# A hybrid decoder trunk on one core: the inverse's small matmuls in another order, and the first loads and token sums arranged anew

## The chip, the cores and the metric

The kernel runs on one core of a Trainium2 chip. Times are device microseconds of one execution; the time before is the median of three runs. A core has TensorE (PE; its weight loads are shown as PEld), VectorE (DVE), ScalarE (ACT), GpSimd (POOL) and SyncE (SP), which here issues nearly all loads and stores. Each engine has its own list of instructions.

## The reference

Two layers act on x of 512 tokens by 1024 features, in fp32. What one layer computes:

```python
h = rms_norm(x, norm_mix[i])
proj = einsum('bsd,dc->bsc', h, w_in[i])            # split into 15 column groups
y_a = gated_delta_net(...)       # 4 heads of 64: causal convolution over 4 tokens, chunked delta rule
y_b = mlstm(...)                 # 4 heads of 64: matrix memory with exponential gates
y_c = sliding_window_attention(q, k, v, sinks, cos, sin)   # 8 query heads, 2 kv heads, window 128
x = x + einsum('bsc,cd->bsd', concatenate([y_a, y_b, y_c]), w_out[i])
u = einsum('bsd,df->bsf', rms_norm(x, norm_mlp[i]), w_up[i])
x = x + einsum('bsf,fd->bsd', square(relu(u)), w_down[i])
gate = sigmoid(einsum('bsd,de->bse', rms_norm(x, norm_ple[i]), w_ple_gate[i]))
x = x + gate * einsum('bsk,kd->bsd', p[i], w_ple_proj[i])
# after both layers: rms_norm(x, norm_final)
```

The gated delta net solves, for each head and chunk, a unit lower triangular system with (I + strict_lower(beta k k^T * decay)), and then carries a 64 x 64 state from chunk to chunk. The attention turns the first 16 of 64 features of q and k by cos and sin of position times frequency (the rotary tables).

## The kernel before

x is kept with features on partitions, as eight tiles X of 128 features by 512 tokens. Every large fp32 product is done as three fp32r matmuls (`mm3`, lines 187 to 193): both operands are split into a rounded high part and the remainder, and high by high, high by low, low by high are added in PSUM. The weights come from HBM as raw tiles of 128 x 512, four stationary blocks each; `w_load_` (line 161) loads one (two buffers), ACT copies it to `whi` (line 167), DVE subtracts to get `wlo` (line 169). `w_ahead` and `w_next` keep two such tiles in flight. RMSNorm is applied late: the matmuls run on x times the gain, and the factor of each token (the row tile R) is multiplied in when a product leaves PSUM.

A layer goes through these sections, in program order:

- tok (lines 391 to 416): the token-major columns (values, gates). For each of 8 chunks of features, 12 matmuls of 400 columns into four PSUM tiles. In layer 0 each chunk first loads X (line 395) and splits it (line 216/217), and loads its own weight tile (`tok_weights`, line 335) through the ring of two raw buffers.
- the norm's factors: in layer 0 `token_sums` (line 220) loads x once more, token-major, in four tiles of 128 x 1024 from a pool of two, and ACT squares and sums them; `Norm.finish` (line 254) makes the reciprocal root on DVE and spreads it with four transposes to R.
- in layer 0 then `rope_tables2` (line 296): the angles, a Sin on ACT, eight transposes on TensorE, and two stores of the tables to HBM, from which section rope reads them.
- gates, rows, cols: gate functions and their running sums; conv (lines 516 to 537): six projections with the convolution; nrmk, vb, decay: norms, and the matrices At (lines 573 to 610).
- binv and dbl (lines 615 to 689): the triangular inverse of 16 blocks (4 chunks of 128 tokens by 4 heads). The 16 x 16 diagonal blocks are solved on DVE; the 32 x 32, 64 x 64 and 128 x 128 levels come from products Y - Y A Y on TensorE. The 32-level uses `t1p` and `y1p` (lines 642, 649), four quadrants of 32 rows by 16 blocks; the 64-level uses `t2p`, `y1p` and `x1p` (lines 668, 673, 676). These are plain fp32 matmuls of 32 x 32 by 32 columns; each shows as two matmul instructions.
- scan (line 694 on): the state passes through four chunks, ending in On.
- mlproj, ml, mlfin: the mLSTM; rope and swa: the attention (yc); og: output gates.
- ycb, out1, ya, out2: `out_group` (line 986) multiplies by w_out. Group one takes yc and the mLSTM's part yb (six stationary blocks for each of 8 output tiles, 144 matmuls), group two the delta net's part ya (two blocks, 48 matmuls). After group two each output tile is split for the MLP and squared for the next norm (`fin_mlp`).
- the MLP in four groups of 8 up and 8 down tiles, and the gated input embedding; the last layer ends with the final norm and the stores.

The order on each engine is not written by hand. A planner takes the instructions in program order and places each when its operands and a buffer should be ready by its model; `tc.high_priority(offset=n)` moves what stands inside it n places ahead in that order (or back, if negative). `seg(name)` applies the table `PRI`; the weight preparation has its own offset, `HPRI` = 250. Within the mixing part the big projections thus fill in between the dependent steps of the three head groups.

At the very beginning one fp32 matmul of zeros (line 137) runs on TensorE before the data are there.

Of the kernel before, what the change touches and what calls it, by code (L numbers as in the profile page):

```python
# [79 lines left out]
def trunk(ctx, tc, xT, xK, pT, posr, pos, wfm, wtm, consts, negi, smalls, gfin, out, dbg=None, depth=L):  # L80
# [51 lines left out]
    with tc.high_priority(offset=4000):  # L132
        zt = tp.tile([128, T], F32, tag="acc", name="zt", bufs=1)
        G.memset(zt, 0.0)
        pw = ps_tile([128, T], "pw")
        for _ in range(1):
            PE.matmul(out=pw, lhsT=zt[:, 0:128], rhs=zt, start=True, stop=True)
# [23 lines left out]
    def w_load_(i):  # L161
        raw = wp.tile([128, WC * 128], F32, tag="raw", name="raw", bufs=2)
        nc.sync.dma_start(out=raw, in_=wfm[i // NCH, i % NCH])
        keep = i >= total - TAILC
# [68 lines left out]
    class Norm:  # L233
# [20 lines left out]
        def finish(self, pt_=None, ps=None):  # L254
            pt_ = pt_ or ps_tile
            ps = self.sums(pt_) if ps is None else ps
            ms = pad(tp, [128, NB], "ms", "ms", 2)
            V.tensor_scalar(ms, ps, 1.0 / D, EPS, ALU.mult, ALU.add)
            rT = pad(tp, [128, NB], "rT", "rT", 2)
            rsqrt(rT, ms, [128, NB], tp, "rn")  # L260
            pr = pt_([128, T], "rb")
            for b in range(NB):
                row_of(pr[:, b * 128:(b + 1) * 128], rT[:, b:b + 1])
            R = tp.tile([128, T], F32, tag="R", name="R", bufs=1)
            A.activation(out=R, in_=pr, func=ACTF.Copy)
# [996 lines left out]
```

## Time and profile before

| what | value |
|---|---|
| median of 3 runs | 1384.7 us (1383.63 to 1391.9) |
| the profiled execution | 1385.26 us |
| its span | 1383.5 us |
| TensorE busy | 1353.4 us, 98% |
| VectorE busy | 824.5 us, 60% |
| ScalarE busy | 614.6 us, 44% |
| granted TensorE clock over the span | 0.975 |
| moved by DMA | 131.89 MB, mean 95 GB/s |

In the profile, a line such as "L642 PE MATMUL t1p<-Yd,At" names the line of the kernel, the engine, the operation, the tile written and those read. In a timeline the first number is the start and the second the length, in us from the start of the span; "x4" merges four in a row, and the brackets say how long the engine had been idle and what ended it. Matmuls overlap: one lasts longer than the distance to the next, so a rate is read from the starts. In a table by stage the busy time is that of each engine within the stage, with the number of instructions that touch it.

The mixing part of layer 0 ends at about 296 us, its MLP at about 640; the mixing part of layer 1 lies between about 700 and 972.

### The profile page before, as it was taken

How to read it: one execution, taken by the hardware profiler on the slowest of the kernel's cores; microseconds unless marked ns; L12 is line 12 of the kernel's file. 1: busy time of each engine (PE TensorE's matmuls, PEld its weight loads, DVE VectorE, ACT ScalarE, POOL GpSimd, SP SyncE). 2: the span in 40 equal slices, each digit the busy share in tenths (PEclk: the TensorE clock that was granted, in tenths of full speed). 3: DMA queues.
4: the chain of work that ended last, by engine and by line, in shares of the span. 5: the costliest groups of instructions: out<-in, count | busy, mean ns of one | idle time of the engine just before them, and what ended most of it. 6: DMA issues, size and time to landing. Idle time of an engine off the chain costs nothing.

```text
span 1383.5 us, 20187 instructions
## 1 busy us (share of the span) xinstructions
PE 1353.4 (98%) x7348; PEld 1126.2 (81%) x7348; DVE 824.5 (60%) x1751; ACT 614.6 (44%) x1245; POOL 136.3 (10%) x152
## 2 busy tenths in 40 slices
PE   8999999999999999999999999999999999999996
PEld 7778888878888888888898888887888888888886
DVE  5878768674343443455769696788534434444555
ACT  6574464353242342443544736625423424234443
POOL 1023121020000000010212231202000000000110
PEclk9999979999999999999999997999999999999998
DMA  6433311323333333333434331313333333333332
GB/s 222 122 100 88 77 35 44 107 84 99 99 95 96 99 91 100 99 92 94 146 109 115 99 80 35 90 48 98 94 98 100 92 99 99 92 99 93 98 94 90
DMA packets 89172, 131.89 MB, mean 95 GB/s; under 512 B 21600, under 2 KB 30304, under 8 KB 89072
## 3 DMA queue, kind: packets, MB, share of 16 engines
q1 hardware_dynamic: 87984, 129.55, 33.3%
q8 instruction: 58, 0.95, 0.3%
q10 hardware_dynamic: 1088, 1.05, 0.2%
q14 instruction: 42, 0.34, 0.1%
HBM read 125.02 MB, written 5.54 MB: 94 GB/s over the span
## 4 chain that ended last, share of the span: by engine, by line
PE 84%; DVE 9%; ACT 2%; DMA 2%; issue 2%; SPq 0%; DVEq 0%; ACTq 0%
PE down L191 9%; PE down L193 9%; PE down L192 8%; PE up L191 8%; PE up L192 8%; PE up L193 8%; PE proj L191 3%; PE proj L192 3%; PE proj L193 3%; PE gate L191 2%; PE gate L193 2%; PE gate L192 2%; DVE wlo L169 2%; PE outp L192 2%; PE outp L191 2%
## 5 line engine op out<-in xcount | busy, mean ns | idle before, releaser
L167 ACT ACTIVATE whi<-raw 128x512 fp32r<-128x512 f32 x404 | 253.1, 630 | 536.0 <-PE down L192 203.8
L169 DVE TENSOR_TENSOR wlo<-raw,whi 128x512 fp32r<-128x512 f32 x404 | 292.3, 725 | 179.4 <-ACT whi L167 178.6
L191 PE MATMUL down<-hidh,whi 128*128 128x512 f32 x512 | 201.7, 394 | 0.0
L192 PE MATMUL up<-xsl,whi 128*128 128x512 f32 x512 | 199.5, 390 | 2.1 <-DVE xsl L217 2.1
L193 PE MATMUL up<-xsh,wlo 128*128 128x512 f32 x512 | 199.4, 390 | 2.0 <-DVE wlo L169 2.0
L191 PE MATMUL up<-xsh,whi 128*128 128x512 f32 x512 | 199.9, 391 | 0.4 <-ACT whi L167 0.2
L193 PE MATMUL down<-hidh,wlo 128*128 128x512 f32 x512 | 199.4, 392 | 0.0
L192 PE MATMUL down<-hidl,whi 128*128 128x512 f32 x512 | 197.5, 388 | 0.0
L191 PE MATMUL proj<-xsh,whi 128*128 128x512 f32 x304 | 123.9, 407 | 1.3 <-ACT whi L167 1.1
L244 POOL TENSOR_TENSOR acc<-acc,sq 128x512 f32<-128x512 f32 x29 | 39.7, 1369 | 862.5 <-ACT sq L243 857.0
L193 PE MATMUL proj<-xsh,wlo 128*128 128x512 f32 x304 | 123.0, 405 | 0.0
L192 PE MATMUL proj<-xsl,whi 128*128 128x512 f32 x304 | 122.3, 402 | 0.0
L192 PEld LDWEIGHTS up<-xsl,whi 128*128 128x128 f32 x512 | 96.1, 188 | 23.8 <-DVE xsl L217 4.0
L193 PEld LDWEIGHTS up<-xsh,wlo 128*128 128x128 f32 x512 | 96.1, 188 | 23.0 <-DVE wlo L169 3.1
L193 PEld LDWEIGHTS down<-hidh,wlo 128*128 128x128 f32 x512 | 96.1, 188 | 22.5
L191 PEld LDWEIGHTS up<-xsh,whi 128*128 128x128 f32 x512 | 96.1, 188 | 21.7 <-ACT whi L167 1.7
L192 PEld LDWEIGHTS down<-hidl,whi 128*128 128x128 f32 x512 | 96.1, 188 | 21.5
L1056 DVE TENSOR_TENSOR X<-X,down 128x512 f32<-128x512 f32 x64 | 44.0, 687 | 115.2 <-PE down L193 115.2
L191 PEld LDWEIGHTS down<-hidh,whi 128*128 128x128 f32 x512 | 96.2, 188 | 19.3
L1047 DVE SCALAR_TENSOR_TENSOR ha<-up,R 128x512 f32<-128x512 f32 x64 | 44.0, 691 | 90.4 <-PE up L193 87.8
L191 PEld LDWEIGHTS proj<-xsh,whi 128*128 128x128 f32 x304 | 59.1, 194 | 14.3 <-ACT whi L167 1.5
L214 DVE TENSOR_TENSOR hidl<-hf,hidh 128x512 fp32r<-128x512 f32 x64 | 44.2, 691 | 42.9 <-ACT hidh L213 42.9
(362 smaller groups left out, 2182.4 us busy)
## 6 DMA issues: line engine op xcount, KB each, us to landing
raw<-wfm SPq DMA_DIRECT2D x404, 256.0 KB, 2.6
X<-xT SPq DMA_DIRECT2D x16, 256.0 KB, 3.1
raw<-wtm SPq DMA_DIRECT2D x16, 200.0 KB, 3.2
xk<-xK SPq DMA_DIRECT2D x4, 512.0 KB, 5.1
gr<-scr SPq DMA_DIRECT2D x8, 256.0 KB, 4.5
Mr<-scr SPq DMA_DIRECT2D x8, 256.0 KB, 3.4
xd<-X SPq DMA_DIRECT2D x8, 256.0 KB, 2.5
X<-xd SPq DMA_DIRECT2D x8, 256.0 KB, 2.8
```

The costliest lines, as they stand in the source:

```text
L167: A.activation(out=hi, in_=raw, func=ACTF.Copy)
L169: (G if (i % NCH) * WC < WPOOL else V).tensor_tensor(lo, raw, f(hi), ALU.subtract)
L191: PE.matmul(out=ps, lhsT=wh, rhs=ah, start=start and k == 0, stop=False)
L192: PE.matmul(out=ps, lhsT=wh, rhs=al, start=False, stop=False)
L193: PE.matmul(out=ps, lhsT=wl, rhs=ah, start=False, stop=stop and k == n - 1)
L214: V.tensor_tensor(lo, src, f(hi), ALU.subtract)
L244: (G if self.n < 6 else V).tensor_tensor(self.acc, self.acc, q, ALU.add)
L1047: V.scalar_tensor_tensor(a_t, ps, 0.0, R, ALU.max, ALU.mult)
L1056: V.tensor_tensor(X[m], X[m], ps, ALU.add)
```

## The change

Six things are done at once.

1. *Warm-up.* The zero tile is of type fp32r and set by DVE, and nine matmuls of it run instead of one.
2. *Head of layer 0.* X and the token weights are loaded at priority 2500, the token weights into eight tiles (`yq`) that are free at that time instead of the ring of two; two projection weight tiles are then loaded ahead; the token-major x comes last, in eight halves of 128 x 512 into other free tiles (`ms_`, `us`), each squared and summed by itself; DVE adds the two halves. `finish` gets two priorities, for the factors and for R.
3. *Rotary tables.* `rope_tables2` is called after the convolution, at priority -1000, instead of after the norm.
4. *Inverse by quadrants.* In the 32-level the loops are exchanged, so that matmuls in a row lie in the four quadrants in turn; in the 64-level those of the two halves alternate, with `x1p` among them, and the ACT copies of both halves come after all the matmuls.
5. *Output groups.* yb moves from the first group to the second, 96 matmuls each; the weights are packed in that order.
6. *Priorities.* The table PRI is another, mostly for layer 0, partly for layer 1. Small tiles come from a pool of their own (`mq`).

```diff
 PRI = {
-    ("tok", 0): -400, ("vb", 0): -100, ("scan", 0): -600, ("og", 0): 30, ("out1", 0): -400, ("ya", 0): -600,
-    ("nrmk", 0): -600, ("ml", 0): -100, ("conv", 0): 150, ("decay", 0): 30, ("mlproj", 0): -300,
-    ("out2", 0): -100, ("dbl", 0): 30, ("ycb", 0): -600, ("cols", 0): 150, ("gates", 0): -50, ("binv", 0): -300,
-    ("gates", 1): -300, ("cols", 1): -100, ("binv", 1): 100, ("dbl", 1): 600, ("mlproj", 1): 30, ("ml", 1): 30,
-    ("rope", 1): 200, ("og", 1): -100, ("out1", 1): -100, ("ya", 1): 400, ("out2", 1): 200, ("ycb", 1): -50,
-    ("mlfin", 1): 60, ("rows", 1): -600, ("tok", 1): 30, ("decay", 1): 30, ("swa", 1): -50,
+    ("tok", 0): 200, ("scan", 0): -200, ("og", 0): 200, ("out1", 0): -100, ("ya", 0): -50, ("nrmk", 0): 600,
+    ("rope", 0): -300, ("ml", 0): -100, ("conv", 0): 600, ("decay", 0): 200, ("mlproj", 0): 400,
+    ("out2", 0): 100, ("ycb", 0): -400, ("cols", 0): 600, ("gates", 0): 200, ("binv", 0): -300,
+    ("rows", 0): -200, ("ch", 0): 2500, ("rb", 0): 300, ("rtab", 0): -1000, ("chm", 0): 150, ("mlfin", 0): 30,
+    ("gates", 1): 400, ("cols", 1): -100, ("binv", 1): 200, ("dbl", 1): 600, ("mlproj", 1): 30, ("ml", 1): 30,
+    ("rope", 1): -400, ("og", 1): -100, ("out1", 1): 150, ("ya", 1): -400, ("out2", 1): 200, ("ycb", 1): -50,
+    ("vb", 1): -600, ("mlfin", 1): 60, ("rows", 1): -600, ("tok", 1): 200, ("decay", 1): 30, ("swa", 1): -1000,
+    ("ple", 1): -200, ("nrmk", 1): 300,
 }
...
-        zt = tp.tile([128, T], F32, tag="acc", name="zt", bufs=1)
-        G.memset(zt, 0.0)
+        zt = tp.tile([128, T], F32R, tag="acc", name="zt", bufs=1)
+        V.memset(f(zt), 0.0)
         pw = ps_tile([128, T], "pw")
-        for _ in range(1):
+        for _ in range(9 or 1):
             PE.matmul(out=pw, lhsT=zt[:, 0:128], rhs=zt, start=True, stop=True)
...
-    def token_sums(raw):
-
-        ss = pad(tp, [128, NB], "sst", "sst", 1)
+    def token_sums(raw, small):
+
+        s2 = small([128, NB, 2], "sst2")
         for b in range(NB):
-            x_b = raw([128, D], "xk")
-            nc.sync.dma_start(out=x_b, in_=xK[b])
-            A.activation(out=x_b, in_=x_b, func=ACTF.Square, accum_out=ss[:, b:b + 1])
+            for j in range(2):
+                x_b = raw(b)([128, T], "xk")
+                nc.sync.dma_start(out=x_b, in_=xK[b, :, j * T:(j + 1) * T])
+                A.activation(out=x_b, in_=x_b, func=ACTF.Square, accum_out=s2[:, b, j:j + 1])
+        ss = small([128, NB], "sst")
+        V.tensor_tensor(ss, s2[:, :, 0], s2[:, :, 1], ALU.add)
         return ss
...
-    def tok_weights(l, k):
-        with hp_():
-            raw = wp.tile([128, WC * 128], F32, tag="raw", name="raw", bufs=2)
+    def tok_weights(l, k, us=None):
+        with hp_(2500 if us else HPRI):
+            raw = f(us("raw")) if us else wp.tile([128, WC * 128], F32, tag="raw", name="raw", bufs=2)
...
             if l == 0:
-                with hp_():
+                with hp_(2500):
                     nc.sync.dma_start(out=X[k], in_=xT[k])
                     XS[k] = split(X[k], xs, "xs", 18, s_l[:, S_GMIX + k:S_GMIX + k + 1])
-            tok_mm(pst, k, *tok_weights(l, k))
-        with hp_():
-            rT, rI, R = (nrm or Norm(False)).finish(pa_tile, None if nrm else token_sums(ws))
+            tok_mm(pst, k, *tok_weights(l, k, yq if l == 0 else None))
         if l == 0:
-            rope_tables2(us, tt)
+            with hp_(2500):
+                w_ahead(2)
+        rT, rI, R = (nrm or Norm(False)).finish(pa_tile, None if nrm else lambda: token_sums(lambda b: (ms_ if b < 3 else us), tt), PRI.get(("rb", l), HPRI),
+                                                PRI.get(("ch", l), HPRI))
...
+        if l == 0:
+            seg('rtab')
+            rope_tables2(us, tt)
+            seg()
         seg('nrmk')
...
-        for q in range(4):
+        q_u = [(q, u) for u in range(16) for q in range(4)]
+        p_u = [(p, u) for u in range(16) for p in range(2)]
+        for q, u in q_u:
             qs = slice(32 * q, 32 * q + 32)
-            for u in range(16):
-                PE.matmul(out=tp_[qs, u, :], lhsT=At[u // 4][qs, u % 4, qs], rhs=Yd[qs, u, :], start=True, stop=True)
+            PE.matmul(out=tp_[qs, u, :], lhsT=At[u // 4][qs, u % 4, qs], rhs=Yd[qs, u, :], start=True, stop=True)
...
-        for p in range(2):
-            lo_, hi_ = slice(64 * p, 64 * p + 32), slice(64 * p + 32, 64 * p + 64)
-            for u in range(16):
-                PE.matmul(out=t2p[lo_, u, :], lhsT=At[u // 4][hi_, u % 4, lo_], rhs=YB[hi_, u, :], start=True, stop=True)
+
+        lohi = [(slice(64 * p, 64 * p + 32), slice(64 * p + 32, 64 * p + 64)) for p in range(2)]
+        for p, u in p_u:
+            lo_, hi_ = lohi[p]
+            PE.matmul(out=t2p[lo_, u, :], lhsT=At[u // 4][hi_, u % 4, lo_], rhs=YB[hi_, u, :], start=True, stop=True)
+        for lo_, hi_ in lohi:
             A.activation(out=t2s[lo_], in_=t2p[lo_], func=ACTF.Copy)
...
-            for u in range(16):
+        for u in range(16):
+            for lo_, hi_ in lohi:
                 PE.matmul(out=y1p[lo_, u, :], lhsT=XB[lo_, u, :], rhs=t2s[lo_, u, :], start=True, stop=True)
+            PE.matmul(out=x1p[32:64, u, :], lhsT=t2s[0:32, u, :], rhs=XB[0:32, u, :], start=True, stop=True)
+        for lo_, hi_ in lohi:
             A.activation(out=Y[lo_, :, hi_], in_=y1p[lo_], func=ACTF.Copy, scale=-1.0)
...
-        out_group(yc + yb, None)
+        out_group(yc, None)
...
-        out_group(ya, fin_mlp)
+        out_group(yb + ya, fin_mlp)
...
-        for ks in ((4, 5, 6, 7, 2, 3), (0, 1)):
+        for ks in ((4, 5, 6, 7), (2, 3, 0, 1)):
             ts += stationary(wo, ks, range(8))
```

More of the change, by code (lines that the diff above doesn't have):

```diff
@@ L163, in w_load_ @@
         nc.sync.dma_start(out=raw, in_=wfm[i // NCH, i % NCH])
-        keep = i >= total - TAILC
+        keep = i >= total - (TAILC)
         pool, th, tl, bh, bl = (xs, "xs", "xs", 18, 18) if keep else (wp, "whi", "wlo", 3, 4)
@@ L252, in sums, with finish @@
             return ps
-        def finish(self, pt_=None, ps=None):
+        def finish(self, pt_=None, ps=None, rb=0, ch=0):
             pt_ = pt_ or ps_tile
[L256 to L265, printed above, removed]
+            with tc.high_priority(offset=ch):
+                ps = self.sums(pt_) if ps is None else ps()
+                ms = pad(tp, [128, NB], "ms", "ms", 2)
+                V.tensor_scalar(ms, ps, 1.0 / D, EPS, ALU.mult, ALU.add)
+                rT = pad(tp, [128, NB], "rT", "rT", 2)
+                rsqrt(rT, ms, [128, NB], tp, "rn")
+            with tc.high_priority(offset=rb):
+                pr = pt_([128, T], "rb")
+                for b in range(NB):
+                    row_of(pr[:, b * 128:(b + 1) * 128], rT[:, b:b + 1])
+                R = tp.tile([128, T], F32, tag="R", name="R", bufs=1)
+                A.activation(out=R, in_=pr, func=ACTF.Copy)
             ri = pad(tp, [128, NB], "ri", "ri", 2)
@@ L296, in rope_tables2 @@
     def rope_tables2(us, small):
-        pi = small([128, NB], "pi").bitcast(I32)
+        pi = small([128, NB], "pi", tag="gl8").bitcast(I32)
         nc.sync.dma_start(out=pi, in_=pos)
@@ L360, in trunk @@
         mp = mix.enter_context(tc.tile_pool(name=f"mp{l}", bufs=1))
+        mq = mix.enter_context(tc.tile_pool(name=f"mq{l}", bufs=1))
         def tt(shape, name, bufs=1, tag=None, dt=F32):
-            return pad(mp, shape, tag or name, name, bufs, dt)
+            return pad(mq if int(np.prod(shape[1:])) % 64 else mp, shape, tag or name, name, bufs, dt)
         def us(shape, name):
@@ L645, in trunk @@
         yp_ = ps_tile([128, 16, 32], "y1p")
-        for q in range(4):
+        for q, u in q_u:
             qs = slice(32 * q, 32 * q + 32)
-            for u in range(16):
-                PE.matmul(out=yp_[qs, u, :], lhsT=Xd[qs, u, :], rhs=ts_[qs, u, :], start=True, stop=True)
+            PE.matmul(out=yp_[qs, u, :], lhsT=Xd[qs, u, :], rhs=ts_[qs, u, :], start=True, stop=True)
         V.tensor_tensor(YB, YB, yp_, ALU.subtract)
@@ L1038, in trunk @@
         HB = 38
-        rT, rI, R = nrm.finish()
+        rT, rI, R = nrm.finish(None, None, PRI.get(("rbm", l), 0), PRI.get(("chm", l), 0))
         XG = [None] * 8
@@ L1065, in trunk, with ple @@
         pS = [split(praw[:, k, :], hp, "pS", 4) for k in range(2)]
+        def ple(m):
+            pq = mm_tile("ple")
+            mm3(pq, pS, True, True)
+            return pq
         rT, rI, R = nrm.finish()
@@ L1092, in trunk @@
             outs = []
-            w_t = [w_next() for _ in range(10 * (8 - HALF))]
+            nw = 10
+            w_t = [w_next() for _ in range(nw * (8 - HALF))]
+            pq_t = None
             for hf in range(2):
@@ L1215, in pack @@
             ts += stationary(wd, range(8 * g, 8 * g + 8), range(8))
-        wg, wpp = a(w_ple_gate)[l], a(w_ple_proj)[l]
+        wg = a(w_ple_gate)[l]
         for m in range(8):
```

13 lines of the change are left out of this document (4 added, 9 removed).

## Prediction

> **What bounds the kernel now.** I read the page first: engines, granted clock, chain of waits.
>
> ```profile
> span 1383.5 us, 20187 instructions
> ...
> PE 1353.4 (98%) x7348; PEld 1126.2 (81%) x7348; DVE 824.5 (60%) x1751; ACT 614.6 (44%) x1245; POOL 136.3 (10%) x152
> ...
> PEclk9999979999999999999999997999999999999998
> ...
> PE 84%; DVE 9%; ACT 2%; DMA 2%; issue 2%; SPq 0%; DVEq 0%; ACTq 0%
> ```
>
> TensorE is busy for 98% of the span and carries 84% of the chain, so time can only come from three places: matmuls that get cheaper, holes of TensorE, and stretches in which it runs at half clock. The table by stage shows where those are (columns: length, busy time and count of PE, PEld, DVE, ACT, POOL, then granted clock, DMA share, GB/s).
>
> ```profile
> 5.00:9.00 4.00, 3.57 (x11) 3.55 (x12) 2.20 (x4) 2.17 (x4) 0.00 (x0) 1.00 1.00 332
> 9.00:13.00 4.00, 4.00 (x19) 3.99 (x18) 3.78 (x6) 3.99 (x8) 0.00 (x0) 1.00 1.05 393
> ...
> 75.00:90.00 15.00, 12.92 (x55) 10.24 (x54) 12.55 (x32) 13.43 (x35) 2.17 (x3) 0.89 0.32 90
> 160.00:216.00 56.00, 54.59 (x671) 48.38 (x670) 32.86 (x100) 33.21 (x102) 10.30 (x16) 0.76 0.21 54
> ...
> 275.00:296.00 21.00, 18.63 (x79) 13.52 (x77) 18.10 (x23) 12.26 (x22) 7.15 (x5) 1.00 0.25 70
> 296.00:640.00 344.00, 344.00 (x1515) 283.36 (x1515) 156.95 (x244) 129.43 (x207) 6.52 (x5) 1.00 0.35 97
> 830.00:895.00 65.00, 65.00 (x761) 56.54 (x760) 42.38 (x125) 42.73 (x131) 10.86 (x18) 0.87 0.22 60
> 948.00:972.00 24.00, 21.56 (x92) 15.82 (x90) 20.57 (x26) 14.54 (x25) 7.15 (x5) 1.00 0.26 76
> ```
>
> The MLP (296 to 640) has no hole: 1515 matmuls in 344 us, 227 ns each. The change leaves it alone. The block inverse of layer 0 lies in 160 to 216, that of layer 1 in 830 to 895, and these stages have the low clocks, 0.76 and 0.87. The ends of the two mixing parts (275 to 296, 948 to 972) have holes: 2.37 and 2.44 us.
>
> **The change part by part.** *The head.* Timeline of before:
>
> ```profile
> 1.31 2.08 PE L137 MATMUL pw<-zt 128*128 128x512 f32 x2 [1.31 <-POOL zt L134]
> ...
> 4.65 0.72 ACT L216 ACTIVATE xsh<-X,sm 128x512 fp32r<-128x512 f32 x1
> ...
> 5.41 0.75 DVE L217 SCALAR_TENSOR_TENSOR xsl<-X,sm,xsh 128x512 fp32r<-128x512 f32 x1 [0.29 <-ACT xsh L216]
> ...
> 5.43 0.70 PE L349 MATMUL tok<-whi,xsh 128*128 128x400 f32 x1 [2.04 <-ACT xsh L216]
> ...
> 6.21 0.54 ACT L340 ACTIVATE whi<-raw 128x400 fp32r<-128x400 f32 x1 [0.83 <-DMA raw<-wtm]
> ...
> 6.78 0.57 DVE L342 TENSOR_TENSOR wlo<-raw,whi 128x400 fp32r<-128x400 f32 x1 [0.62 <-ACT whi L340]
> ...
> 9.60 1.53 PE L349 MATMUL tok<-whi,xsh 128*128 128x400 f32 x4
> ...
> 10.93 0.94 PE L350 MATMUL tok<-wlo,xsh 128*128 128x400 f32 x4
> ...
> 19.73 0.88 PE L349 MATMUL tok<-whi,xsh 128*128 128x400 f32 x4
> ...
> 25.55 0.45 PE L350 MATMUL tok<-wlo,xsh 128*128 128x400 f32 x1 [1.25 <-DVE wlo L342]
> ...
> 29.27 0.60 PE L326 MATMUL prt<-cst,rsrc 128*128 128x128 f32 x4
> ...
> 29.70 0.60 PE L231 MATMUL rb<-cst,rT 128*128 128x128 f32 x4
> ...
> 30.06 0.47 PE L191 MATMUL proj<-xsh,whi 128*128 128x512 f32 x1
> ```
>
> Layer 0's token matmuls, 8 chunks of 12, start at 5.43 and the first projection at 30.06: 24.6 us. Four in a row take 1.53 us at 9.60 and 0.88 us at 19.73; less the length of the last, that is 333 and 180 ns apiece, so up to about 10.9 us TensorE ran at half speed. Needed were 96 x 0.18 = 17.3 us and 12 transposes (prt, rb) at (29.70 - 29.27) / 4 = 0.11, so 1.3 us: 6.0 us were lost. Some 16 matmuls at half speed (10.93 - 5.43 over 0.333) cost 16 x 0.153 = 2.5 us of it, waits for weights the other 3.5 (1.25 of it at 25.55).
>
> After: nine warm-up matmuls in fp32r. The fp32 one was two instructions; a token one is one, so 512 columns at the half-speed rate cost 0.333 x 512 / 400 = 0.43 us, nine 3.8 us. From about 1.3 they end at 5.1, ahead of the first data at 5.43, and block nothing. Before, full speed came 5.5 us after steady work began; counted from 1.3 that is 6.8, so only (6.8 - 5.43) / 0.333 = 4 matmuls stay slow, 0.6 us. Loads: a chunk of X and of token weights (128x512 and 128x400 f32) is 456 KB, 1.2 to 1.4 us at the 332 to 393 GB/s above; per chunk ACT needs 0.72 + 0.54, DVE 0.75 + 0.57 us, and TensorE 12 x 0.18 = 2.16. TensorE is the slowest, so with eight weight tiles free at once instead of a ring of two its waits go. Tokens end at 5.43 + 17.3 + 0.6 = 23.3, rb at 23.7; the eight prt transposes (0.9) are still paid, later. Gain 30.06 - 23.7 - 0.9 = **5.5 us**. The token sums leave the front of the load queue (SP), which lets the projection's weights pass them; they are done on ACT in eight halves beside the tokens. Bounds: +9 (nine warm-ups at the fp32 price, 9 x 2.08 = 18.7 us, keep TensorE from the tokens to 20; the 2.5 + 3.5 lost us come back) and -6.6.
>
> *The inverse.* The busy time of the four tiles t1p, y1p, t2p, x1p over both layers (150 to 216 and 830 to 895), in this order; then t1p alone, first in the middle of one quadrant and then where the next begins; then a pair that changes array halves already:
>
> ```profile
> sum 131.00, PE 8.29; mean PE 4.15
> ...
> sum 131.00, PE 14.81; mean PE 7.41
> ...
> sum 131.00, PE 4.77; mean PE 2.39
> ...
> sum 131.00, PE 2.57; mean PE 1.28
> ...
> 164.55 4.14 PE L642 MATMUL t1p<-Yd,At 32*32 32x32 f32 x128
> ...
> 164.90:165.03 0.14, 0.14 (x10) 0.14 (x8) 0.00 (x0) 1.00 0.00 0
> 165.45:165.59 0.14, 0.14 (x14) 0.14 (x11) 0.00 (x0) 1.00 0.00 0
> ...
> 104.31 0.49 PE L594 MATMUL pkq<-kT 64*128 64x128 f32 x4
> ...
> 105.40 0.50 PE L191 MATMUL proj<-xsh,whi 128*128 128x512 f32 x1
> ```
>
> That is 30.4 us for 832 instructions (256, 384, 128, 64; two for each matmul in fp32), 37 ns each; t1p at full clock takes 4.14 / 128 = 32. In 0.135 us four new ones start within a quadrant (10 records are touched, six of them from before, since one lasts about six spacings), and eight where one quadrant's end meets the next one's start: 16 ns. So two quadrants do run side by side. The pkq rows agree more weakly: 16 of them from 104.31 to 105.40, 68 ns against 108 for the full-height transposes. The change puts the neighbours of t1p and the first y1p in four quadrants in turn, the rest in two or three. I take the 16 ns that the trace shows: 832 x 16 = 13.3 us, 17.1 saved. The ends are 8 ns (four at a time, -23.8) and 32 (no overlap, only the half-clock share goes, -3.8). Against it: the ACT copies of t2p and y1p now come after both halves instead of beside the second; other matmuls are queued there (TensorE is busy 54.59 of 56 us), and where they run out it costs some 3 us. I take **-14**.
>
> The Trainium skill, page "TensorE: Matmul & The Clock Gate" (section on why 56 ns is not 53), says that matmul starts never come closer than about 25 ns, however small. By it, an estimate, 832 x 25 = 20.8 us would remain and 9.6 be saved. The trace disagrees: its 16 ns are below that floor.
>
> *The two output groups.* mLSTM's part yb moves from the first to the second: 96 and 96 matmuls a layer instead of 144 and 48. Rows of the old ending, and of the output matmuls before and after 254 us (layer 0) and 920 us (layer 1):
>
> ```profile
> 269.96 0.69 DVE L994 TENSOR_TENSOR X<-X,outp 128x512 f32<-128x512 f32 x1 [1.59 <-PE outp L193]
> ...
> 270.57 0.68 DVE L169 TENSOR_TENSOR wlo<-raw,whi 128x512 fp32r<-128x512 f32 x1
> ...
> 200.00:254.00 54.00, 21.17 (x77) 14.66 (x78) 2.74 (x4) 0.88 0.22 64
> ...
> 880.00:920.00 40.00, 11.83 (x43) 7.45 (x44) 1.36 (x2) 1.00 0.25 73
> ...
> 252.29 0.82 PE L1017 MATMUL pty<-cst,On 128*128 128x128 f32 x6
> ```
>
> Per block of the last group DVE needs 0.69 (X) + 0.75 (split) + half a weight tile, 0.34 = 1.78 us, TensorE 6 x 0.227 = 1.36: DVE paces, hence the holes, 4.8 us in all. With twelve matmuls it is 2.12 against 2.72, and TensorE paces. I take **-4**, as the first up matmuls still wait for the last split. The cover: 48 matmuls, 10.9 us a layer, are no longer there to fill in ahead of the scan's end. When its result is transposed (252.29) 77 output matmuls had been issued, in layer 1 43 by 920; the new first group has 96, so the filler lasts, and a shortage would cost at most that 10.9.
>
> *Clock.* 160:216 at 0.76 and 830:895 at 0.87 lose 56 x 0.24 + 65 x 0.13 = 22 us of full-speed time. The inverse's 14 us are 12% of these 121: **-2.5**; bounds 0 and -22.
>
> *Priorities, rotary tables, pools.* The tables' Sin and transposes go behind the convolution and are needed only by the rope; DVE and ACT do the same work. In layer 0 convolution (600) and mLSTM projections (400) are now pulled further ahead than the weight preparation (250), which they were not. Nearest row: 75:90, where ACT is busy 13.43 of 15 us and TensorE loses 2.08, 14%. If 60 to 160 ran so, +14; a better order gains at most the small holes, some -10. What the tables take along lies in the same range: on ACT a table load,
>
> ```profile
> 20.23 1.28 ACT L316 ACT_TABLE_LOAD   x1
> ```
>
> and one to go back, 2.6 us if the convolution waits for both; two POOL memsets, and on SP a small load and two 256 KB writes, which the projection's weight loads are queued behind. The rope, which stands behind the mLSTM heads in the program, reads them. I take 0 for all of it.
>
> **Sum.** -5.5 - 14 - 4 - 2.5 = -26. The profiled execution took 1385.3 us (span 1383.5), 0.6 over the median 1384.7: 1385.3 - 26 = **1359**.
>
> **Rivals.** *Dependent steps bind:* the seven steps of the inverse hand over through ACT and DVE, filler is missing, and the saved time becomes holes; the inverse gives 3.8, the clock nothing: 1385.3 - 5.5 - 3.8 - 4 = 1372. Against it: TensorE is busy 65.00 of 65 us in layer 1's stage. *Weights late:* the +14 above, 1373. *Issue floor:* the inverse saves 9.6 less 3, which gives 1366. *Clock falls, slower than before:* the half clock comes while TensorE is busy all the time but with small matmuls, so busy records do not hold it up. Denser small matmuls and less wide filler could hold 160:216 and 830:895 at half: 56 x (0.76 / 0.5 - 1) + 65 x (0.87 / 0.5 - 1) = +77 at worst, two thirds of it 1359 + 51 = 1410; it decides from +40. The Trainium skill (same page, "What's actually happening") has half rate after an idle window of about 3.4 us; by that rule it needs holes, and this trace shows half clock without them, so I keep the case. *The order isn't kept* (the planner puts the matmuls back in rows of one quadrant): 1371 to 1376.
>
> **Numbers.** Forecast 0.58, own range 1345 to 1371. Better than that (four quadrants at a time, 10 more, the small holes, 10: about 1338) 0.10. Dependent steps 0.10, weights late 0.06, issue floor 0.05, order not kept 0.02, clock 0.09. About 1% (13.8 us) is what a measurement can tell from no change: faster means under 1370.9, slower over 1398.5. Faster: 0.54 + 0.10 + 0.05 + 0.01 = 0.70; slower 0.10, nearly all of it the clock; same 0.20. Range: from the better case, 1334, to past the late weights with a lost head, 1387.
>
> **What would show it.** Head: first projection at 23 to 25 us, token matmuls 180 ns apart from about 7 us. Inverse: t1p's 128 in 2 us or less instead of 4.14, four tiles together near 13 us. Ending: no waits of up for DVE worth over 1 us, and 6 to 10 us more between the scan's transposes and the MLP. Clock: 0.8 or more in both inverse stages. It is wrong if t1p keeps 32 ns, if holes take the place of the saved time, or if the low clock spreads.

## The result, and the profile after

The changed kernel takes 1369.3 us (1367.5 to 1370.4, four runs) beside 1386.2 us of the kernel before (1383.6 to 1391.9, four runs): a ratio of 0.9871, 95% interval 0.9837 to 0.9905. It is faster by 1.3%, some 17 us instead of the 26 that the sum gave; 1359 was 10 us too low, and the measured time lies inside the range. The profiled execution took 1370.4 us. Of all executions below, two lie far from the rest of their kernels (7030 us with the tables in the head, 2189 us with the quadrants alone); without them the medians would be at most 0.2 us lower.

The page of the kernel after: span, busy time, granted clock in 40 slices, chain by engine.

```profile
span 1368.6 us, 20217 instructions
...
PE 1322.1 (97%) x7355; PEld 1101.2 (80%) x7355; DVE 812.8 (59%) x1753; ACT 614.9 (45%) x1253; POOL 134.5 (10%) x151
...
PEclk9969999999999999999999999999999999999998
...
PE 81%; DVE 11%; ACT 4%; DMA 2%; issue 2%; SPq 0%; POOL 0%; DVEq 0%; ACTq 0%; POOLq 0%
```

TensorE's busy time fell by 31 us (1353.4 to 1322.1), the span by 15. The rest, 16 us, came back as TensorE being idle (30.1 us before, 46.5 after), and the chain gives a first hint: its shares on DVE and ACT rose from 9 to 11% and from 2 to 4%. The low slices of the two inverses (6 and 25 of before) are gone; a new one has come, the third. The table by stage, of after (columns as in the prediction):

```profile
65.00:100.00 35.00, 19.25 (x71) 14.72 (x71) 19.51 (x51) 19.47 (x46) 2.90 (x6) 0.66 0.15 46
...
160.00:216.00 56.00, 54.67 (x750) 45.65 (x751) 47.72 (x123) 39.16 (x120) 19.98 (x24) 0.97 0.30 86
275.00:296.00 21.00, 21.00 (x95) 17.38 (x94) 13.84 (x21) 11.89 (x20) 5.93 (x5) 1.00 0.35 99
...
830.00:895.00 65.00, 62.70 (x851) 52.15 (x851) 51.73 (x165) 40.72 (x125) 15.61 (x21) 1.00 0.28 80
933.00:957.00 24.00, 24.00 (x111) 19.99 (x109) 16.73 (x26) 14.07 (x23) 7.00 (x5) 1.00 0.33 88
```

The inverse stages run at 0.97 and 1.00, and both endings (275:296, and 933:957, which answers to 948:972) are without a hole. But 65:100 is new: 19.25 us busy of 35 at a clock of 0.66, where the same 35 us of the kernel before read

```profile
65.00:100.00 35.00, 32.92 (x139) 26.74 (x140) 26.07 (x61) 28.05 (x72) 12.06 (x15) 0.89 0.43 122
```

TensorE is idle for 15.75 us there, 13.7 more than before; this is called the hole from here on. It shows in the ends of the layers. The last norm sum of layer 0's mixing part starts at 296.3 us before and at 296.7 after: layer 0 gained nothing. From there to the same point of layer 1 it is 675.8 us before and 660.3 after: all that the kernel gained lies in layer 1.

The inverse itself, after: the busy time of t1p, y1p, t2p and x1p over both layers (150 to 225 and 822 to 880; one row for each tile, in this order), then t1p and what follows it in the timeline.

```profile
sum 133.00, PE 2.57; mean PE 1.29
...
sum 133.00, PE 4.97; mean PE 2.49
...
sum 133.00, PE 2.40; mean PE 1.20
...
sum 133.00, PE 2.39; mean PE 1.19
...
170.46 1.29 PE L659 MATMUL t1p<-Yd,At 32*32 32x32 f32 x128
171.67 0.39 PE L918 MATMUL psc<-skh,sqS 128*128 128x256 f32 x1
```

Together 12.3 us instead of 30.4; as y1p and x1p of the 64-level now run side by side and are each counted in full, TensorE spends 10.0 us on the four. The 128 instructions of t1p take (171.67 - 170.46) / 128 = 9.5 ns each, where they took 32.

The head, after: TensorE's timeline, then SP's queue from its second issue on.

```profile
1.45 4.21 PE L139 MATMUL pw<-zt 128*128 128x512 f32 x9 [1.45 <-DVE cvec L462]
8.73 0.70 PE L357 MATMUL tok<-whi,xsh 128*128 128x400 f32 x1 [3.07 <-ACT xsh L218]
9.23 0.54 PE L358 MATMUL tok<-wlo,xsh 128*128 128x400 f32 x1
...
12.89 1.53 PE L357 MATMUL tok<-whi,xsh 128*128 128x400 f32 x4
14.23 1.01 PE L358 MATMUL tok<-wlo,xsh 128*128 128x400 f32 x4
...
28.76 0.39 PE L193 MATMUL proj<-xsh,whi 128*128 128x512 f32 x1
```

```profile
1.19 0.89 SPq L165 DMA_DIRECT2D raw<-wfm  x2
2.13 0.43 SPq L346 DMA_DIRECT2D raw<-wtm  x1
2.60 0.43 SPq L406 DMA_DIRECT2D X<-xT  x1
```

The two projection weight tiles, which in the program's text stand behind X and the token weights, were put ahead of them in the queue; all have the priority 2500. The first token matmul starts at 8.73 instead of 5.43 (an experiment below shows that these two loads are the reason). The nine warm-up matmuls ended at 5.66 (5.1 was worked out), but 3.07 us of idle time follow, and the token matmuls then stand 333 ns apart until about 14.2. The first projection came at 28.76; 23.7 was worked out.

### The profile page after: what moved, and what is told of

The parts are those of the page before. It is cut to its first block, busy times and chain, and to the rows that moved or that the text cites. A ratio compares the mean times of both kernels' runs of the same rounds, so it can differ in the third digit from the quotient of the medians.

```text
span 1368.6 us, 20217 instructions
## 1 busy us (share of the span) xinstructions
PE 1322.1 (97%) x7355; PEld 1101.2 (80%) x7355; DVE 812.8 (59%) x1753; ACT 614.9 (45%) x1253; POOL 134.5 (10%) x151
## 4 chain that ended last, share of the span: by engine, by line
PE 81%; DVE 11%; ACT 4%; DMA 2%; issue 2%; SPq 0%; POOL 0%; DVEq 0%; ACTq 0%; POOLq 0%
PE up L194 9%; PE up L195 8%; PE down L195 8%; PE down L194 8%; PE up L193 8%; PE down L193 8%; PE proj L194 2%; PE proj L193 2%; PE proj L195 2%; PE gate L193 2%; PE gate L194 2%; PE gate L195 2%; PE outp L194 2%; PE outp L195 2%; PE outp L193 2%
## 5 line engine op out<-in xcount | busy, mean ns | idle before, releaser
L249 POOL TENSOR_TENSOR acc<-acc,sq 128x512 f32<-128x512 f32 x29 | 39.4, 1358 | 844.6 <-ACT sq L248 844.6
```

The costliest lines, as they stand in the source:

```text
L249: (G if self.n < 6 else V).tensor_tensor(self.acc, self.acc, q, ALU.add)
```

## The experiments

All runs in one table. Times are medians; the ratio is to the kernel before, timed on the same chip in between (its own median moved between 1386 and 1392, so the ratio carries it). The last two columns are from the profiled execution, which can lie off the median (for "before + quadrants" it took 1368.0 us, for "layer 0's old priorities" 1387.3): the start of layer 0's last norm sum, and the time from there to the same point of layer 1.

| kernel | us | ratio, 95% interval | layer 0 | to layer 1 |
|---|---|---|---|---|
| before | 1386.2 | 1 | 296.3 | 675.8 |
| after | 1369.3 | 0.9871 (0.9837 to 0.9905) | 296.7 | 660.3 |
| tables in the head | 1373.3 | 0.9892 (0.9858 to 0.9927) | - | - |
| layer 0's old priorities | 1382.0 | 0.9951 (0.9925 to 0.9977) | 304.2 | 669.8 |
| prt in the other PSUM pool | 1364.4 | 0.9834 (0.9801 to 0.9867) | 293.5 | 658.1 |
| projection weights later | 1364.8 | 0.9836 (0.9809 to 0.9864) | 291.4 | 660.2 |
| no rotary tables | 1367.7 | 0.9824 (0.9803 to 0.9846) | 296.4 | 658.4 |
| before + quadrants | 1372.4 | 0.9849 (0.9819 to 0.9879) | 284.9 | 670.3 |
| weights later + prt | 1361.6 | 0.9785 (0.9760 to 0.9811) | 289.6 | 658.7 |
| weights later + tables in head | 1377.6 | 0.9896 (0.9871 to 0.9920) | 292.0 | 669.9 |
| the same as "weights later + prt", solve's priority | 1361.6 | 0.9791 (0.9767 to 0.9816) | 289.1 | 659.2 |
| before + quadrants + output groups | 1363.0 | 0.9806 (0.9781 to 0.9831) | 281.3 | 665.5 |
| after without quadrants | 1388.9 | 0.9995 (0.9968 to 1.0023) | 305.4 | 669.1 |
| weights later + prt, half solve | 1361.6 | 0.9803 (0.9757 to 0.9848) | 287.7 | 658.1 |

**Where does TensorE wait in 65:100?** Its waits there, after, and its timeline from the end of one row of projections to the start of the next:

```profile
PE pt L580 <- DVE vT L542: 8.0, 2, 4.5
PE pss L548 <- ACT sqq L546: 3.7, 1, 3.7
PE proj L193 <- ACT whi L169: 2.5, 1, 2.5
PE proj L193 <- DVE craw L531: 1.4, 1, 1.4
```

```profile
76.78 0.95 PE L548 MATMUL pss<-cst,sqq 128*128 128x2 f32 x8
81.39 1.87 PE L548 MATMUL pss<-cst,sqq 128*128 128x2 f32 x8 [3.65 <-ACT sqq L546]
86.81 0.66 PE L580 MATMUL pt<-cst,vT 128*128 128x128 f32 x2 [3.56 <-DVE vT L542]
91.93 0.69 PE L580 MATMUL pt<-cst,vT 128*128 128x128 f32 x2 [4.45 <-DVE vT L542]
92.72 1.08 PE L333 MATMUL prt<-cst,rsrc 128*128 128x128 f32 x4
...
96.87 0.77 PE L193 MATMUL proj<-xsh,whi 128*128 128x512 f32 x1
97.45 0.63 PE L194 MATMUL proj<-xsl,whi 128*128 128x512 f32 x1
97.87 0.63 PE L195 MATMUL proj<-xsh,wlo 128*128 128x512 f32 x1
```

The two largest waits are for ends of the convolution (vT, sqq), which the kernel before had too. What is missing is filler: from 76.8 to 96.9 there isn't one projection between them. The projections write to the two PSUM buffers `mm`, and the transposes `prt` of the rotary tables, moved here by the change, write to the same two. Half clock comes with the hole: the projections at 96.87 stand 0.43 us apart, at full clock 0.23.

*Tables back in the head* (the call of `rope_tables2` where it was, all else as changed):

```diff
+        if l == 0:
+            rope_tables2(us, tt)
         dump(f"R{l}", R)
...
-        if l == 0:
-            seg('rtab')
-            rope_tables2(us, tt)
-            seg()
         seg('nrmk')
```

> The changed kernel with only the rotary tables back in the head, right after the norm's factors, without a priority of their own. The changed kernel gained nothing by the start of layer 0's MLP (its norm sums stand at 295.99 us, before at 295.63), although its inverse and its head are shorter; TensorE idles most between 65 and 100 us. Theory T (the moved tables): the two Sin table loads on ACT and the eight transposes, which hold the two projection PSUM tiles while they wait, make that hole. Then the hole between 65 and 100 shrinks by more than half, layer 0's norm sums come at 278 to 286 us and the kernel takes 1353 to 1360 us. Theory P (the new order of layer 0 on ACT: the decay exponentials stand ahead of the convolution's tanh): the hole stays, norm sums at 292 or later, 1366 us or more.

Measured: 1373.3 us, no better than the change itself. There are no rows of the hole for this kernel; a run further down, with the weights later as well, has them.

*Layer 0's old priorities* (the table PRI for layer 0 as before, with the new entries ch, rb, rtab and chm kept):

```diff
-    ("tok", 0): 200, ("scan", 0): -200, ("og", 0): 200, ("out1", 0): -100, ("ya", 0): -50, ("nrmk", 0): 600,
...
+    ('tok', 0): -400,
+    ('vb', 0): -100,
+    ('scan', 0): -600,
...
```

> The changed kernel with the priorities of layer 0 that the kernel before had (those of the new names ch, rb, rtab, chm kept, so the tables stay behind the convolution). Theory P (the new order of layer 0 makes the hole): the hole between 65 and 100 us shrinks by more than half, layer 0's norm sums come at 278 to 286 us and the kernel takes 1353 to 1360 us. Theory T (the moved tables): the hole stays in some form, norm sums at 292 or later, 1366 us or more.

Measured: 1382.0 us, worse by 12.7, and the hole stays as it was:

```profile
65.00:100.00 35.00, 19.11 (x76) 14.79 (x74) 21.04 (x57) 18.50 (x56) 8.64 (x13) 0.64 0.18 60
```

So the new priorities of layer 0 didn't make the hole. Between the profiled executions, which are 16.9 us apart, 7.5 us lie in layer 0 and 9.5 in layer 1 (660.3 to 669.8), whose text is the same. Its order is not: of some 620 VectorE instructions between 700 and 960 us, nearly all stand at another place than in the run "weights later + prt" (over 1200 differing lines of both lists); in the run "weights later" few do (under 100 lines). The planner had made another plan of layer 1 out of an edit in layer 0.

*prt in the other PSUM pool:*

```diff
-            pt = mm_tile("prt")
+            pt = pa_tile([128, T], "prt")
```

> The changed kernel with the tables where it puts them, but their eight transposes write a PSUM tile of the other pool of four instead of one of the two that the projections use. Theory T in its PSUM form (the projections have no PSUM tile while the transposes wait for their input): projections run on between 82 and 97 us, norm sums of layer 0 at 280 to 288, 1355 to 1362 us. If it is the ACT table loads or the order instead: projections still stand still there, within 3 us of the changed kernel's 1369.

Measured: 1364.4 us. Projections run on between 82 and 97 us, as expected by theory T in its PSUM form; the time and layer 0's end (293.5) are later than it said. Its windows:

```profile
65.00:100.00 35.00, 28.43 (x116) 23.02 (x117) 21.81 (x55) 25.67 (x59) 3.14 (x6) 0.85 0.23 75
...
168.00:216.00 48.00, 44.25 (x698) 35.66 (x697) 37.70 (x100) 33.84 (x103) 14.80 (x18) 0.96 0.36 100
216.00:296.00 80.00, 74.46 (x420) 60.87 (x420) 61.31 (x165) 29.66 (x57) 8.19 (x7) 0.96 0.23 67
```

The hole shrinks from 15.75 to 6.6 us with only the pool of the transposes changed: that the projections stood behind the shared buffers is shown. But 168:216 has 3.75 idle and 216:296 has 5.5, where the change has 0.67 and 0.47. Of 9.2 us won, 8.1 are lost later in the same layer.

*Projection weights later* (`w_ahead(2)` at 250 instead of 2500):

```diff
-            with hp_(2500):
+            with hp_():
                 w_ahead(2)
```

> The changed kernel with the two projection weight tiles of the head loaded at the usual weight priority instead of 2500. In the changed kernel these two loads stand first in the load queue, and the first token matmul starts at 8.73 us instead of 5.43. Theory H (those two loads, 512 KB, delay the head): the first token matmul starts at 5 to 6 us and the first projection 2 to 3 us earlier than the changed kernel's 28.9 to 29; but if the hole between 65 and 100 sets the end of layer 0's mixing part, the whole gains less than 1.5 us: 1367 to 1369. If layer 0 passes the head on, 1365 to 1367.

Measured: 1364.8 us. Its head:

```profile
1.45 4.21 PE L139 MATMUL pw<-zt 128*128 128x512 f32 x9 [1.45 <-DVE cvec L462]
5.75 0.68 PE L357 MATMUL tok<-whi,xsh 128*128 128x400 f32 x1
...
6.46 0.34 PE L357 MATMUL tok<-whi,xsh 128*128 128x400 f32 x1
6.64 0.34 PE L358 MATMUL tok<-wlo,xsh 128*128 128x400 f32 x1
...
23.38 0.39 PE L193 MATMUL proj<-xsh,whi 128*128 128x512 f32 x1
```

This is the head that the prediction described: no gap after the warm-up, 180 ns apart from 6.46, first projection at 23.38 (23.7 was worked out). The 5.4 us (28.76 to 23.38) are passed on in full to the end of layer 0 (296.7 to 291.4), and 4.5 to the whole. The hole is still there (busy 20.42 of 35), so it doesn't keep an earlier head from counting.

*No rotary tables* (the angles, Sin and transposes are left out and constants stored in their place, so the attention isn't rotated):

```diff
-        A.activation(out=k, in_=r, func=ACTF.Sin)
...
             tab = us([128, T], "rtab")
-            A.activation(out=tab, in_=pt, func=ACTF.Copy)
+            G.memset(tab, 1.0 - j)
```

> The changed kernel without the work of the rotary tables: no angles, no Sin, no transposes; two tiles of ones and zeros are stored in their place, so the attention is not rotated. This bounds what the tables can cost where the change puts them. Theory T (they make the hole between 65 and 100 us and with it layer 0's loss): norm sums of layer 0 at 278 to 286 instead of 296, 1352 to 1360 us. If the hole is the convolution's own chain over ACT and DVE, which was there before: the hole shrinks by a third at most, 1364 to 1369.

Measured: 1367.7 us, layer 0's end at 296.4; neither theory has both. The hole is filled as far as with prt elsewhere (29.39 of 35 busy), and the time comes back later: 216:296 is busy 73.60 of 80 and 168:216 43.12 of 48. Even without any work for the tables layer 0 ends no earlier: the tables are what makes the hole, not what makes the layer long.

*The quadrants alone, on the kernel before* (the whole block from t1p to x1p as in the change, nothing else):

```diff
-        for q in range(4):
+        q_u = [(q, u) for u in range(16) for q in range(4)]
...
+        for q, u in q_u:
             qs = slice(32 * q, 32 * q + 32)
-            for u in range(16):
-                PE.matmul(out=tp_[qs, u, :], lhsT=At[u // 4][qs, u % 4, qs], rhs=Yd[qs, u, :], start=True, stop=True)
+            PE.matmul(out=tp_[qs, u, :], lhsT=At[u // 4][qs, u % 4, qs], rhs=Yd[qs, u, :], start=True, stop=True)
...
```

> The kernel before with the inverse by quadrants alone (the matmuls in turn over the quadrants, the copies after both halves). In the changed kernel the four tiles take 9.4 us instead of 28.3, all starts counted. Theory Q (TensorE sets the pace in both layers, so cheaper matmuls count in full): norm sums of layer 0 8 to 11 us earlier, those of layer 1 18 to 23, 1362 to 1368 us. Theory C (layer 0 is set by its chain through DVE and ACT, as in the changed kernel): layer 0 gains under 4 us, layer 1 8 to 12, 1371 to 1376.

Measured: 1372.4 us. One of six parts gives, within the intervals, as much as the whole change. Layer 0 ends at 284.9, 11.4 earlier, about as theory Q had it; layer 1 gains only 5.5 more, and the time is the one of theory C. Neither holds for both layers.

*Weights later and prt elsewhere, together:*

```diff
-            pt = mm_tile("prt")
+            pt = pa_tile([128, T], "prt")
...
-            with hp_(2500):
+            with hp_():
                 w_ahead(2)
```

> The changed kernel with two edits at once: the head's two projection weight tiles at the usual priority, and the tables' transposes in the other PSUM pool. Each alone gave 1364 to 1365. If they add, 5 and 5: 1359 to 1361. If layer 0 is set by the chain from the norm factors on, only the earlier head counts: 1362 to 1366.

Measured: 1361.6 us, ratio 0.9785, the lowest here (three others lie within its interval). The gains add up in part: 7.7 us by the medians, of 4.5 and 5.0. Its two largest waits between 130 and 296 us:

```profile
PE proj L195 <- DVE wlo L171: 4.2, 2, 2.7
PE pty L1035 <- DVE On L766: 2.9, 1, 2.9
```

They hang on a weight tile that VectorE hadn't split yet, and on the scan's last result (the numbers are us in total, times, and the longest).

*Weights later, and the tables in the head:*

```diff
-            with hp_(2500):
+            with hp_():
                 w_ahead(2)
...
+        if l == 0:
+            rope_tables2(us, tt)
         dump(f"R{l}", R)
...
-        if l == 0:
-            seg('rtab')
-            rope_tables2(us, tt)
-            seg()
```

> The changed kernel with the head's two projection weight tiles at the usual priority and the tables back in the head. The tables in the head alone gave 1370 to 1373, the later weights alone 1364 to 1365. Its profile shows whether the hole between 65 and 100 us is there without the tables. Theory T: no hole over 6 us there. If the chain of the convolution makes it: 10 us or more of hole remain. Time 1363 to 1368.

Measured: 1377.6 us, later than expected. But the hole is gone, as theory T had it:

```profile
65.00:100.00 35.00, 30.40 (x135) 24.05 (x134) 25.20 (x64) 26.92 (x70) 4.95 (x7) 0.90 0.33 98
```

4.6 us of idle time are left of 14.6 with the weights later alone. This is the third way of taking the tables out of the projections' way that fills the hole, and the third that doesn't make layer 0 shorter by as much. Layer 0 ends at 292.0, nearly as with the weights later alone (291.4), but layer 1 takes 669.9 instead of 660.2 in another plan (some 700 differing lines on VectorE, counted as above). The 12.8 us by which it is slower are mostly this, so the time says little on the tables.

*Is it then the block solve on VectorE?* Both runs start from the kernel with weights later and prt elsewhere. With the hole filled, the 16 steps from Ab to Xb take 42 us (126.7 to 168.9) instead of 21.6 before, and t1p starts at 182.4 instead of 164.6. Theory B was that this chain now sets the end.

```diff
-    ("out2", 0): 100, ("ycb", 0): -400, ("cols", 0): 600, ("gates", 0): 200, ("binv", 0): -300,
+    ("out2", 0): 100, ("ycb", 0): -400, ("cols", 0): 600, ("gates", 0): 200, ("binv", 0): 300,
```

> The kernel with the token sums' R and the projection weights later and the rope transposes in the other PSUM pool (1361.6 us), with one number changed: the priority of layer 0's 16-step block solve goes from -300 to +300, so that its small VectorE steps no longer stand behind VectorE's other work. Theory B (once the hole at 65-100 us is filled, layer 0 ends by the chain through VectorE's solve: Ab loaded at 126.7, last step at 168.9, 42 us where the kernel before takes 21.6): the solve takes under 26 us, t1p starts at 160 to 168 us instead of 182, the layer's norm sums end at 278 to 284 us instead of 289.6, and the kernel takes 1349 to 1356 us. Rival (TensorE's and VectorE's work in sum sets the end, and the steps put behind become late instead): the solve gets short, but the norm sums end at 287 us or later and the kernel takes 1359 us or more.

Measured: 1361.6 us and nothing moved. The first steps and the last one of the solve in VectorE's timeline:

```profile
128.96 0.18 DVE L638 TENSOR_TENSOR px<-Ab,px 128x16 f32<-128x16 f32 x1 [1.33 <-DMA Ab<-scA]
...
129.27 0.68 DVE L171 TENSOR_TENSOR wlo<-raw,whi 128x512 fp32r<-128x512 f32 x1
129.87 0.18 DVE L638 TENSOR_TENSOR px<-Ab,px 128x32 f32<-128x32 f32 x1
...
167.93 0.57 DVE L640 TENSOR_REDUCE px<-px 128x16 f32<-128x256 f32 x1
```

The planner still sets other work between two steps: the number changed nothing in VectorE's order. The run can't tell B from its rival.

*Half the solve:*

```diff
-        for i in range(16):
+        def solve_step(i):
...
+        for i in range(16 if l else 8):
             solve_step(i)
+        if l == 0:
+            V.tensor_scalar(Xb[:, 8:16, :], prod[:, 8:16, :], -1.0, None, ALU.mult)
...
         A.activation(out=Yd, in_=YB, func=ACTF.Copy, scale=sc[:, 5:6])
+        for i in range(16 if l else 8, 16):
+            solve_step(i)
```

> The priority of the run before left VectorE's order as it was, so it couldn't tell. Here the chain itself is cut, in the kernel with R's transposes in the other PSUM pool and the projection weights later (1361.6 us): in layer 0 the inverse of a block uses 8 of its 16 rows from the solve and unit rows for the rest; the other 8 steps are still computed, with the same instructions, but after what hangs on them (they are left out of the result, so layer 0's inverse is another one). VectorE's and TensorE's work stays the same. Theory B (with the hole at 65-100 us filled, the chain through VectorE's solve sets layer 0's end): t1p starts at 158 to 166 us instead of 182, TensorE's idle time between 130 and 296 us falls from 11 us to under 6, the layer's norm sums end at 282 to 286 us instead of 289.6, and the kernel takes 1353 to 1358 us. Rival (the idle time has another cause, or moves on): t1p starts as early, but TensorE stays idle for 9 us or more, the norm sums end at 288 us or later, and the kernel takes 1360 us or more.

Measured: 1361.6 us, layer 0's end at 287.7. Only part of the cut took effect. scX was stored at 140.6 instead of 169.0, but

```profile
172.92 0.72 ACT L657 ACTIVATE Yd<-YB,cst 128x512 f32<-128x512 f32 x1
```

came right after the last of the steps moved behind (172.8): Yd is the fifth tile of a ring of four, the first of which is Ab, so it couldn't be written before these steps had read Ab. t1p started at 174.5, 8 us earlier instead of 20. Still, the last matmul of the inverse (y2q) starts at 211.0 us in both, so these 8 us were lost within the inverse, and the layer gained 1.9. TensorE is idle for 11.4 us between 130 and 296 us, not less than the 10.7 without this edit, as the rival had it. That speaks against B in its simple form and, as the chain was cut only in part, doesn't settle it.

*Quadrants and output groups on the kernel before:*

```diff
...
-        out_group(yc + yb, None)
+        out_group(yc, None)
...
-        out_group(ya, fin_mlp)
+        out_group(yb + ya, fin_mlp)
...
-        for ks in ((4, 5, 6, 7, 2, 3), (0, 1)):
+        for ks in ((4, 5, 6, 7), (2, 3, 0, 1)):
```

> The kernel before with the inverse by quadrants and with the new output groups, the old head and the old order (with the quadrants alone it took 1372.4 us). Forecast's term (-4 us for the output groups, some 2 us per layer): 1366 to 1370 us, and the holes of VectorE before the end of the output projections, 2.4 us per layer, gone. Rival (the holes only move, or the wait for the last block grows as 43 of 96 products are left behind it): 1371 to 1376 us.

Measured: 1363.0 us, 9.4 less than with the quadrants alone by the medians, 6 by the ratios (the two were timed beside different runs of before). TensorE is busy 43.00 of 43 us in 905:948, the end of layer 1's mixing part, instead of 40.46 with the quadrants alone. Two of the six parts beat all six (0.9806 and 0.9871, intervals apart).

*All but the quadrants* (the block from t1p to x1p as it was before):

```diff
...
-        for q, u in q_u:
+        for q in range(4):
             qs = slice(32 * q, 32 * q + 32)
-            PE.matmul(out=tp_[qs, u, :], lhsT=At[u // 4][qs, u % 4, qs], rhs=Yd[qs, u, :], start=True, stop=True)
+            for u in range(16):
+                PE.matmul(out=tp_[qs, u, :], lhsT=At[u // 4][qs, u % 4, qs], rhs=Yd[qs, u, :], start=True, stop=True)
...
```

> The changed kernel with the old inverse (one quadrant after the other), all else as changed: what head, order, tables and output groups give alone. If the parts add up (quadrants alone 14 to 19 us, all together 17 to 21): 1384 to 1388 us, no gain without the quadrants, and layer 0's norm sums end at 302 to 308 us. If the head's 5.5 us and the output groups' 4 us of the forecast are there but the inverse's part is lost in layer 0: 1374 to 1379 us, with layer 0's norm sums at 296 to 299 us.

Measured: 1388.9 us, ratio 0.9995: without the quadrants the change gives nothing. The clock in 160:216 is 0.94 here, though: all else as changed raises it from 0.76 without the quadrants, too.

## Why the prediction was right, and where it wasn't

The side and the range held, the range in part by luck. The quadrants with the clock and the output groups were to give 20.5 us and gave some 27 on the old order; the other parts were to give 5.5 and cost some 9 beside that kernel (0.9871 against 0.9806). Two errors, of some 6 and some 14 us, lay on opposite sides. By its steps:

- **The inverse, -14.** Right in mechanism, a little short in size. 832 instructions at 16 ns made 13.3 us; measured are 12.3 by the tiles, and 10.0 with what runs side by side counted once. Starts in four quadrants come 9.5 ns apart, not the 16 of two that the trace of before could show. Whether the copies behind both halves cost the 3 us set aside for them was not measured by itself. With the clock, the quadrants are worth 0.9995 - 0.9871 = 1.2%, 17 us, with all else as changed (19.5 by the medians), and 1.5%, 21 us, on the kernel before; forecast were 16.5 with the clock's term. The issue floor of about 25 ns that the Trainium skill gives (page "TensorE: Matmul & The Clock Gate", section on why 56 ns is not 53) isn't seen here for 32 x 32 matmuls in different quadrants.
- **The clock, -2.5.** Right in direction, and the size was a guess: 0.76 and 0.87 became 0.97 and 1.00. Counted as the prediction counts, 56 x 0.21 + 65 x 0.13 = 20 of the 22 us of full-speed time came back, not 2.5. How much of the measured time this is worth was not isolated, and in layer 0 it isn't the quadrants' alone (0.94 without them). The rival that denser small matmuls would hold TensorE at half clock didn't come.
- **The output groups, -4.** The holes went as worked out (21.00 of 21 and 24.00 of 24). On top of the quadrants alone they gave more than 4, 6 to 9 us; where the surplus comes from was not isolated. The test "6 to 10 us more between the scan's transposes and the MLP" was wrong: from the last of these transposes to the last norm sum it takes 1.5 us more in layer 0 (36.2 against 34.7) and 4.7 in layer 1 (41.6 against 36.9). It had left out that much of the old first group stood in that stretch too: 77 of its 144 matmuls had been issued by 254 us, 43 by 920.
- **The head, -5.5.** It failed by the order of the loads: the first projection came 1.3 us earlier than before (28.76 against 30.06), not 6.4. The step that failed reads "The token sums leave the front of the load queue (SP), which lets the projection's weights pass them": they passed X as well. With them later the step's own numbers come out (5.75, 6.46, 23.38), and the gain arrives.
- **Priorities, rotary tables, pools, 0 with -10 to +14.** The 0 was wrong in both layers, with opposite signs. Beside the kernel with quadrants and output groups alone, the changed one ends layer 0 later by 15.4 us (296.7 against 281.3), with its first projection at about the same time (28.8 against 29.0); in layer 1 it needs 5.2 us less (660.3 against 665.5). By the medians the changed kernel takes 6.4 us more in all. The loss of layer 0 is just past the +14 of the bound. It was right that something would hold TensorE between 60 and 160; it wasn't the weights (2.5 of 15.6 us), as the rival had it. The prediction asked what work the tables take along and named queues of ACT, POOL and SP, but not the two PSUM buffers that their transposes share with the projections, TensorE's filler.
- The test that it is wrong "if holes take the place of the saved time" came half true. In layer 0 they did.

Layer 0 isn't longer for having more work. Up to 280 us the kernel with quadrants and output groups alone and the changed one read, in this order:

```profile
0.00:280.00 280.00, 264.76 (x1855) 219.42 (x1856) 215.75 (x566) 156.88 (x379) 54.05 (x69) 0.96 0.34 103
...
0.00:280.00 280.00, 254.84 (x1794) 211.93 (x1795) 205.88 (x557) 151.12 (x375) 50.42 (x66) 0.94 0.33 98
```

TensorE is idle 9.9 us more in the changed kernel, and the lower clock costs about 5 us more (0.02 of 280, rounded): together nearly all of the 15.4 us.

What stays open is where that idle time comes from. Layer 0 doesn't go below 287.7 us in any kernel with the new head, neither with the hole filled and the head early (23.0 us idle up to 280) nor without the tables' work, while the old head with the two other parts ends at 281.3 in spite of a first projection 5.5 us later. The new head with the old order and the tables where they were, which would separate the head from the rest, was not run. Filler used at 65:100 is missing later (layer 0's last projection ends at 225.3 us after, at 197.5 in the kernel with both repairs), and the solve gets slower among it; that either of them sets the end is argued, not shown. Layer 0 of the kernel with two parts and layer 1 of the changed one would, if they added up, come to about 1358 us; that was not tried.

## What to carry to other kernels

Small matmuls that fill one quadrant of the array should be issued with the quadrants in turn: the new order of these matmuls took t1p's from 32 to 9.5 ns each here and was worth the whole change. When work is moved, list the buffers that it takes along as well as its instructions; a few transposes in the PSUM ring of the big products shut out the filler for 20 us. And in a kernel whose order a planner makes, time each part alone on the old order: six parts together hid that two of them gave more than all.

## What the runs showed of the hardware

- Nine warm-up matmuls were worth nothing when a pause of 3.07 us followed. Full speed came 5.5 us after the first token matmul (8.73 to 14.2), as in the kernel before with its one warm-up matmul (5.43 to 10.9). Without the pause it came 5.0 us after the warm-up began (1.45 to 6.46). How long it takes differs from run to run: in the kernel without the quadrants, whose head is the same text, the nine took 3.77 us instead of 4.21, so the last of them ran at full speed already, and after a pause of 3.64 us the token matmuls stood 333 ns apart again. The Trainium skill (page "TensorE: Matmul & The Clock Gate", section "What's actually happening") speaks of about 3.4 us of sustained work, in a window that runs freely; the traces agree, as their records of the granted clock change only at whole multiples of 3.41 us, and the change to full speed came at the end of such a step that TensorE had worked through (7.6 to 11.0 us before, 11.1 to 14.5 after). Work that starts between two such ends first has to see out the step that is running.
- In these stretches the column of the granted clock can't be relied on. The row of after

```profile
9.00:13.00 4.00, 4.00 (x13) 3.95 (x14) 3.54 (x6) 2.70 (x5) 0.35 (x1) 1.00 1.06 372
```

gives 1.00 where the same matmul stands 333 ns apart that takes 180 later. The trace's record of the clock begins only with the change to full speed, at 14.5 us; before that, the distance of the starts shows the speed.
- Busy records don't say whether the clock is kept up. The inverse stage of layer 0 is as full after (54.67 of 56 us) as before (54.59), with the clock at 0.97 instead of 0.76. In the kernel before, 3.41 us that are filled by t1p's 32 x 32 matmuls without a gap are followed by 3.41 us at half clock:

```profile
164.64:168.06 3.42, 3.42 (x120) 3.42 (x121) 2.27 (x5) 1.01 (x2) 0.00 (x0) 1.00 0.29 79
168.06:171.47 3.41, 3.41 (x28) 3.35 (x24) 0.76 (x2) 1.67 (x4) 0.00 (x0) 0.50 0.29 79
```

Layer 1 has the same pair (840.48 to 843.89 and 843.89 to 847.30). After the change t1p is through in 1.3 us, and the clock stays at 1.00 over it and the next 3.41 us (168.09 to 174.91). Low clocks come with idle time too, as in 65:100 (0.66).
